# Decoder layer on one Trainium2 core: scratch tiles for two pairs, a token-shift mix on ScalarE, and convolution splits and evacuations at high priority

## The chip, the core and the metric

The kernel runs on one core of a Trainium2 chip. The metric is the device time of one execution, in microseconds. TensorE (PE) does the matrix products, VectorE (DVE), ScalarE (ACT) and GpSimd (POOL) the elementwise work, and the queue of SyncE (SP) issues nearly all loads.

## The reference, cut to what matters

One layer of a decoder on 256 prompt tokens and 8 sequences of 4 new tokens (288 columns in all). The part that matters here:

```python
proj = h @ w_in                                   # columns: r, k, v, then bg, cg, hc
rkv = p_rkv + (p_rkv_prev - p_rkv) * mu_rkv       # mix with the token before
decay = exp(-exp(w_log)); a = sigmoid(...)        # two small low-rank products
kk = k * k_k / max(|k * k_k|, 1e-12)
k = k * (1 + (a - 1) * k_a)
y, S = wkv7_scan(state, r, decay, k, v, kk, kk * a)    # delta rule, 16 heads
zc = causal_dwconv(state_conv, cg * hc, conv_w)        # width 3
o_conv = bg * zc
x = x + ga1 * (concat(o_rwkv, o_conv) @ w_out)
# then a gated feed-forward part and a last norm
```

## The kernel before, in words

Activations lie with features on the 128 partitions and 288 tokens in the free dimension. Every large product is made of three passes (`mm3`, lines 163 to 166): a piece of weights of 1 MB (`raw`) is split into a high part (`whi`, a cast on ScalarE, line 154) and a low part (`wlo`, a subtraction on VectorE, line 156), and TensorE does high x high, high x low and low x high, 128x288 each. There are four tiles for `raw` in the stage that matters here and three each for `whi` and `wlo`.

The kernel has these stages: setup and the r, k, v columns of `w_in` (to about 268 us), then the stage of this change, then the scan for eight pairs of heads (`second(p)`), then `w_out`, the feed-forward part and the end.

The stage of this change (lines 555 to 731) goes over the eight pairs of heads p. For each it does `lerp` (the mix of r, k and v with the token before, three of them), `first(p)` (the preparation of the scan: line 599 is its product on TensorE), and `blocks_of(p - 1)` (small products, lines 635 and 637, whose results go to memory in HBM as `dN` and `dNs`). All their temporary tiles are turns of rings in one scratch tile, `ws`: two `ldr` tiles for `lerp` and eight `er` tiles for `first`, which uses seven of them for one pair.

Between these, generators are stepped. `cv` is the convolution's own product over 2048 features: 24 steps, each with one piece of 1 MB, two splits and 48 passes of 128x288 (6.3 us by the profile). Two steps make one part, and `conv_evac` then takes the two accumulators out. `rest` is the product for the adaLN vectors that later stages need; one step loads 1 MB and takes four passes of 128x512 side by side (lines 298 and 301).

After the last pair, `substitute()` reads `dN` and `dNs` back, does a forward substitution on VectorE and GpSimd (lines 664 and 665, 31 steps that depend on each other), and writes the result to memory (`dT`, `dTT`, `dTs`). `second(0)` reads that back into `T1` and `TTc` (lines 994 to 998). Then `drain(cv)` runs what is left of the convolution.

The code is ordered by a scheduler: within its program order and priorities it fixes the order of the instructions on each engine before the run, and on the chip each engine keeps to that order.

## Time and profile before

| | |
|---|---|
| median of 3 runs | 1697.93 us (1694.07 to 1701.84) |
| the profiled execution | 1694.01 us, span 1692.2 us |
| TensorE busy | 1630.8 us, 96% of the span |
| VectorE, ScalarE, GpSimd busy | 1160.7, 713.6, 387.1 us |
| TensorE clock granted, mean | 0.983 |

The span is what the trace covers, 1.8 us less than the execution's time. A busy TensorE is not one at its peak, since passes overlap in the records; the number of passes in a stretch tells more. The granted clock is 1.00 at 2.4 GHz and 0.5 at 1.2 GHz, and a value between is a mean over a stretch that had both.

### The profile page before, as it was taken

What the parts mean: (1) busy time and instruction counts of PE and PEld (TensorE: products, weight loads), DVE (VectorE), ACT (ScalarE), POOL (GpSimd) and SP (SyncE); (2) the same over time, 40 slices, a digit from 0 to 9 for tenths busy, and PEclk for the clock granted to TensorE, in tenths of its full rate; (3) what the DMA queues carried; (4) which work ended last, traced back from release to release, by engine and by line L of the source; (5) the groups of instructions that cost most, each with busy time, mean ns of one, the idle gap of its engine ahead of it and who ended that gap; (6) DMA issues with size and microseconds to landing.
All of it is one profiled execution on the core that took longest, in us unless ns stands there. A gap on an engine that the chain in (4) does not pass through costs nothing.

```text
span 1692.2 us, 32395 instructions
## 1 busy us (share of the span) xinstructions
PE 1630.8 (96%) x12713; PEld 1481.5 (88%) x12713; DVE 1160.7 (69%) x2464; ACT 713.6 (42%) x1281; POOL 387.1 (23%) x853
## 2 busy tenths in 40 slices
PE   6999999999889999899899999999999999999996
PEld 3778898889866666699799999999999999999996
DVE  3687798977846665554776676757676766757586
ACT  4543355444234433333654343443434343434444
POOL 2132011221633232100143031221213131221212
PEclk9999999999979999999999999999999999999998
DMA  8897865688567667954654545545545445445532
GB/s 274 287 334 270 281 214 191 198 254 258 160 181 248 215 232 247 331 175 141 224 175 150 175 157 168 174 152 173 163 162 174 151 150 183 166 156 169 174 125 76
DMA packets 238306, 333.61 MB, mean 197 GB/s; under 512 B 35698, under 2 KB 180826, under 8 KB 229546
## 3 DMA queue, kind: packets, MB, share of 16 engines
q1 hardware_dynamic: 234937, 324.55, 58.8%
q0 software_dynamic: 2848, 6.20, 1.1%
q8 instruction: 100, 1.64, 0.4%
q10 hardware_dynamic: 368, 0.79, 0.2%
q14 instruction: 53, 0.43, 0.1%
HBM read 321.63 MB, written 9.89 MB: 196 GB/s over the span
## 4 chain that ended last, share of the span: by engine, by line
PE 84%; DVE 8%; ACT 3%; DMA 2%; POOL 1%; issue 1%; SPq 0%; DVEq 0%; ACTq 0%
PE acc L164 22%; PE acc L166 22%; PE acc L165 22%; PE ada L298 5%; DVE wlo L156 2%; PE acc L298 2%; ACT whi L154 1%; PE wb L298 1%; PE wa L298 1%; PE acc L301 1%; PE wa L301 1%; PE ada L301 1%; DMA A<-in_x_sample_dram 1%; PE wb L164 1%; PE wb L166 0%
## 5 line engine op out<-in xcount | busy, mean ns | idle before, releaser
L164 PE MATMUL acc<-actH,whi 128*128 128x288 f32 (+1 forms) x2368 | 707.1, 299 | 9.0 <-ACT whi L154 5.2
L165 PE MATMUL acc<-actL,whi 128*128 128x288 f32 (+1 forms) x2368 | 703.6, 297 | 0.1
L166 PE MATMUL acc<-actH,wlo 128*128 128x288 f32 (+1 forms) x2368 | 700.9, 297 | 2.8 <-DVE wlo L156 2.7
L156 DVE TENSOR_TENSOR wlo<-raw,whi 128x1024 fp32r<-128x1024 f32 (+1 forms) x391 | 478.6, 1226 | 217.3 <-ACT whi L154 211.0
L154 ACT CAST whi<-raw 128x1024 fp32r<-128x1024 f32 x400 | 417.6, 1048 | 475.9 <-PE acc L165 409.3
L164 PEld LDWEIGHTS acc<-actH,whi 128*128 128x128 f32 x2368 | 448.6, 189 | 20.2 <-ACT whi L154 9.7
L166 PEld LDWEIGHTS acc<-actH,wlo 128*128 128x128 f32 x2368 | 447.8, 190 | 5.6 <-DVE wlo L156 4.6
L165 PEld LDWEIGHTS acc<-actL,whi 128*128 128x128 f32 x2368 | 448.3, 189 | 0.4 <-DVE actL L161 0.3
L164 PE MATMUL acc<-gH,whi 128*128 128x288 f32 x704 | 209.1, 297 | 1.7 <-DVE rd L1051 1.7
L166 PE MATMUL acc<-gH,wlo 128*128 128x288 f32 x704 | 210.4, 299 | 0.0
L165 PE MATMUL acc<-gL,whi 128*128 128x288 f32 x704 | 205.7, 292 | 0.0
L1144 POOL COPY uO<-ub 128x2 f32<-128x2 f32 x88 | 24.6, 280 | 548.6 <-ACT ub L1142 548.6
L164 PEld LDWEIGHTS acc<-gH,whi 128*128 128x128 f32 x704 | 132.3, 188 | 3.8 <-PE acc L166 3.7
L165 PEld LDWEIGHTS acc<-gL,whi 128*128 128x128 f32 x704 | 134.0, 190 | 0.0
L166 PEld LDWEIGHTS acc<-gH,wlo 128*128 128x128 f32 x704 | 132.0, 187 | 0.7
L1049 DVE SCALAR_TENSOR_TENSOR xT<-acc,modT,xT 128x256 f32<-128x256 f32 x192 | 91.7, 477 | 27.6 <-PE acc L166 27.6
L301 PE MATMUL ada<-raw,cT 128*32 128x512 f32 x576 | 109.3, 623 | 0.0
L298 PE MATMUL ada<-raw,cT 128*32 128x512 f32 x192 | 100.0, 623 | 1.0 <-DMA raw<-in_ada_w_dram 0.7
L1149 DVE SCALAR_TENSOR_TENSOR uz<-ub,cw,uz 128x304 f32<-128x304 f32 x176 | 96.5, 548 | 4.3
L1141 POOL COPY ub<-sF 128x16 f32<-128x16 f32 x88 | 71.2, 809 | 103.9 <-ACT sF L1045 103.9
L1147 DVE TENSOR_SCALAR uz<-ub,cw 128x304 f32<-128x304 f32 x88 | 33.1, 376 | 49.5 <-ACT ub L1143 49.5
L463 DVE TENSOR_TENSOR A<-acc,A 128x296 f32<-128x296 f32 x96 | 44.2, 463 | 29.0 <-PE acc L166 28.5
(449 smaller groups left out, 1985.0 us busy)
## 6 DMA issues: line engine op xcount, KB each, us to landing
raw<-in_ada_w_dram SPq DMA_DIRECT2D x88, 1024.0 KB, 5.2
raw<-in_ffn_up_dram SPq DMA_DIRECT2D x88, 1024.0 KB, 5.1
raw<-in_w_in_dram SPq DMA_DIRECT2D x48, 1024.0 KB, 7.4
raw<-in_ffn_down_dram SPq DMA_DIRECT2D x44, 1024.0 KB, 5.2
raw<-in_w_out_dram SPq DMA_DIRECT2D x16, 1024.0 KB, 5.9
raw<-in_ada_w_dram SPq DMA_DIRECT2D x16, 512.0 KB, 8.0
dX<-xT SPq DMA_DIRECT2D x1, 2304.0 KB, 16.0
xT<-dX POOLq DMA_DIRECT2D x4, 576.0 KB, 9.3
```

The costliest lines, as they stand in the source:

```text
L154: S.copy(hi, raw)
L156: (GP if cur['share'] and cur['turns'] % cur['share'] == 0 else V).tensor_tensor(lo, raw, hi.bitcast(F32), SUB)
L164: E.matmul(acc, wh, xh, start=start, stop=False)
L165: E.matmul(acc, wh, xl, start=False, stop=False)
L166: E.matmul(acc, wl, xh, start=False, stop=stop)
L298: ins = calls[0]().ins
L301: c()
L463: V.tensor_tensor(A[:, t, 2:LW], acc[:, :NL], A[:, t, 2:LW], ADD)
L1049: V.scalar_tensor_tensor(xT[:, t, :T0], acc[:, :T0], modT[:, m, t, 0:1], xT[:, t, :T0], MUL, ADD)
L1141: GP.tensor_copy(bv[:, :, 0:2], sF[:, :, j].rearrange("p (b t) -> p b t", t=2))
L1147: V.tensor_scalar(z[:, :NC - 2], b[:, 0:NC - 2], cw[:, 0, j:j + 1], None, MUL)
L1149: V.scalar_tensor_tensor(z[:, :NC - 2], b[:, t:NC - 2 + t], cw[:, t, j:j + 1], z[:, :NC - 2], MUL, ADD)
```

## The change

It has five parts, all in the stage of the pairs.

- `lerp` computes the mix in another form: (1 - mu) times the tile plus mu times the tile shifted by one. The two multiplications and a small one for the first tokens of the 8 sequences go to ScalarE (lines 583 to 585 of the changed file), one addition stays on VectorE (line 586). The new constant `omur` is made once.
- One scaling in `first` (line 619) and the first tap of the convolution (line 706) go from VectorE to ScalarE.
- The rings `ldr` and `er` have four and sixteen tiles. The ten new ones lie where the substitution's tiles `UL`, `TL` and `TTL` lie.
- The splits of the convolution and its evacuations are placed under `high_priority`, so the scheduler takes them first on their engines.
- The loop over the pairs steps `cv` once and not twice, so 8 of the 24 steps come before `substitute()` in the program and 16 after.

```diff
-            ldr, off = ring(0, (NT,), 2)
-            er, off = ring(off, (NT,), 8)
+            ld_, off = views(0, *[(NT,)] * 2)
+            e_, off = views(off, *[(NT,)] * 8)
...
+            more, _ = views(off + NP * NT, *[(NT,)] * 10)
+            (ocv, UL, TL, TTL, ULs, TTs), off = views(off, (NP, NT), (32, 32), (32, 32), (32, 32), (TS, TS), (TS, TS))
+            ldr, er = turns(ld_ + more[8:]), turns(e_ + more[:8])
...
-                d = ldr()
-                before(d, A[:, t])
-                V.scalar_tensor_tensor(A[:, t, 2:2 + NT], d, murkv[:, t:t + 1], A[:, t, 2:2 + NT], MUL, ADD)
+                a, d, mu = A[:, t], ldr(), murkv[:, t:t + 1]
+                S.activation(d, a[:, 1:1 + NT], AF.Copy, scale=mu)
+                S.activation(s4(d[:, T0:])[:, :, 0], a[:, 2 + NT:LW], AF.Copy, scale=mu)
+                S.activation(a[:, 2:2 + NT], a[:, 2:2 + NT], AF.Copy, scale=omur[:, t:t + 1])
+                V.tensor_tensor(a[:, 2:2 + NT], a[:, 2:2 + NT], d, ADD)
...
-                V.tensor_scalar(a, a, kav[:, p:p + 1], omka[:, p:p + 1], MUL, ADD)
+                S.activation(a, a, AF.Identity, scale=kav[:, p:p + 1], bias=omka[:, p:p + 1])
...
-                                    hv, lv = split(raw[:, kk:kk + 4], 4)
+                                    with tc.high_priority():
+                                        hv, lv = split(raw[:, kk:kk + 4], 4)
...
-                        for n in range(2):
-                            conv_evac(part, 2 * jj + n, accs[n], cg[:, n], z[n])
+                        with tc.high_priority():
+                            for n in range(2):
+                                conv_evac(part, 2 * jj + n, accs[n], cg[:, n], z[n])
...
-                    V.tensor_scalar(z[:, :NC - 2], zb[:, 0:NC - 2], cwv[:, j:j + 1], None, MUL)
+                    S.activation(z[:, :NC - 2], zb[:, 0:NC - 2], AF.Copy, scale=cwv[:, j:j + 1])
...
                 step(cv)
-                step(cv)
```

On TensorE, the place around the products of the last pair (`blocks_of(7)`: lines 635 and 637 before, 645 and 647 in the changed file, where line numbers are up to 12 higher; `ada` is the adaLN product, `acc` a pass of the convolution). Before:

```order
L166 MATMUL acc<-actH,wlo 128x288
L298 MATMUL ada<-raw,cT 32x512
L301 MATMUL ada<-raw,cT 32x512 x3
L298 MATMUL ada<-raw,cT 32x512
L301 MATMUL ada<-raw,cT 32x512 x3
L635 MATMUL wb<-XA,XB 64x64 x4
L637 MATMUL wb<-XA,XB 32x32
L635 MATMUL wa<-XA,XB 64x64 x4
L637 MATMUL wa<-XA,XB 32x32
L164 MATMUL acc<-actH,whi 128x288
```

and in the changed kernel:

```order
L166 MATMUL acc<-actH,wlo 128x288
L299 MATMUL ada<-raw,cT 32x512
L302 MATMUL ada<-raw,cT 32x512 x3
L299 MATMUL ada<-raw,cT 32x512
L302 MATMUL ada<-raw,cT 32x512 x3
L645 MATMUL wb<-XA,XB 64x64 x4
L647 MATMUL wb<-XA,XB 32x32
L645 MATMUL wa<-XA,XB 64x64 x4
L647 MATMUL wa<-XA,XB 32x32
L262 MATMUL ada<-con,ada_sb 128x128 x4
L164 MATMUL acc<-actH,whi 128x288
```

The rows read alike; what moved is the work around them. Before, 768 passes of the convolution stand ahead of these products (96 for each pair) and 384 behind them; now it is 384 ahead (16 to 59 between one pair's products and the next) and 768 behind. The number of `ada` steps ahead of them is 16 in both.

On VectorE and ScalarE, the place where the first pairs' mixes are made, behind the two splits for the low-rank weights. On VectorE before (line 341 the shifted difference, 342 its small part, 576 the mix, 611 and 612 already `first`):

```order
L161 TENSOR_TENSOR wlo<-raw,whi 96x1024 x2
L342 TENSOR_TENSOR ws<-A 128x8 x2
L611 SCALAR_TENSOR_TENSOR ws<-con,XA 128x288
L576 SCALAR_TENSOR_TENSOR A<-ws,vec,A 128x288 x2
L341 TENSOR_TENSOR ws<-A 128x288
L612 TENSOR_TENSOR ws<-ws,XA 128x288
L342 TENSOR_TENSOR ws<-A 128x8
L156 TENSOR_TENSOR wlo<-raw,whi 128x1024
```

and on ScalarE now (583 to 585 the three multiplications of a mix, 607 the first step of `first`):

```order
L154 CAST whi<-raw 128x1024
L583 ACTIVATE ws<-A,vec 128x288 x2
L584 ACTIVATE ws<-A,vec 128x8
L585 ACTIVATE A<-A,omur 128x288
L584 ACTIVATE ws<-A,vec 128x8
L585 ACTIVATE A<-A,omur 128x288
L583 ACTIVATE ws<-A,vec 128x288
L154 CAST whi<-raw 128x1024
L584 ACTIVATE ws<-A,vec 128x8
L585 ACTIVATE A<-A,omur 128x288
L607 ACTIVATE ws<-A,vec 128x288
```

Where VectorE had three instructions for each of the 24 mixes, ScalarE now has three and VectorE one addition.

On SyncE's queue, the place where the last pair's results go out and come back for the substitution (`dN`, `dNs` out: lines 651 and 652; back into `ws`: 658 and 663; `in_w_in` are pieces for the convolution, `in_ada_w` for `rest`). In the changed kernel:

```order
L253 DMA raw<-in_ada_w_dram 128x2048
L651 DMA dNs<-ws 32x4 x2
L170 DMA raw<-in_w_in_dram 128x8x256
L652 DMA dN<-ws 128x4x64
L651 DMA dNs<-ws 32x4 x2
L170 DMA raw<-in_w_in_dram 128x8x256
L658 DMA ws<-dNs 64x16 x2
L663 DMA ws<-dN 32x32x32 x4
L170 DMA raw<-in_w_in_dram 128x8x256 x14
```

Now 14 loads of the convolution stand behind these transfers in the queue; before, there were four. For every two `in_ada_w` pieces of the pairs the queue now has one convolution piece, where before it had two.

## Rows read from the trace of the kernel before

**Rows 1.** The page: span, and busy time of TensorE.

```profile
span 1692.2 us, 32395 instructions
...
PE 1630.8 (96%) x12713; PEld 1481.5 (88%) x12713; DVE 1160.7 (69%) x2464; ACT 713.6 (42%) x1281; POOL 387.1 (23%) x853
```

**Rows 2.** Stretches of the stage: width, busy (instructions), TensorE clock, DMA share, GB/s.

```profile
268.00:300.00 32.00, 28.61 (x213) 25.20 (x212) 31.53 (x71) 22.23 (x43) 6.95 (x14) 1.00 0.60 202
300.00:415.00 115.00, 115.00 (x912) 100.03 (x910) 95.27 (x199) 51.15 (x87) 28.74 (x53) 1.00 0.75 238
415.00:441.00 26.00, 26.00 (x197) 25.84 (x197) 18.97 (x48) 6.68 (x8) 9.89 (x29) 1.00 0.88 254
441.00:466.00 25.00, 20.07 (x128) 19.58 (x127) 23.77 (x53) 8.80 (x11) 17.13 (x33) 0.87 0.27 91
475.00:503.60 28.60, 24.65 (x238) 17.68 (x237) 11.62 (x38) 10.53 (x29) 9.78 (x33) 0.64 0.78 194
```

**Rows 3.** What TensorE waited for, 268 to 512 us: total, times, longest us.

```profile
PE acc L164 <- DVE ws L703: 3.8, 1, 3.8
PE acc L301 <- DMA T<-dT: 2.7, 1, 2.7
PE acc L166 <- DVE wlo L156: 2.7, 2, 1.6
```

**Rows 4.** The chain of waits, 310 to 350 us: start, us, what.

```profile
328.33 0.68 PE wa L599 x2
...
345.37 0.68 PE wb L599 x2
```

**Rows 5.** TensorE in order of time: start, us, line, operation, tiles.

```profile
268.12 0.62 PE L298 MATMUL ada<-raw,cT 128*32 128x512 f32 x1
...
414.88 0.24 PE L637 MATMUL wa<-XA,XB 64*32 64x32 f32 x2
...
475.04 0.62 PE L298 MATMUL ada<-raw,cT 128*32 128x512 f32 x1
...
522.22 0.43 PE L892 MATMUL wa<-AX,ws 128*128 128x64 f32 x2
```

**Rows 6.** The chain of waits, 474 to 512 us.

```profile
474.36 2.06 ACT ws L666
...
476.44 4.21 DMA dT<-ws
...
490.94 0.62 PE wa L892 x2
```

**Rows 7.** Groups of instructions, 268 to 415 us: busy us, mean ns, idle before.

```profile
L156 DVE TENSOR_TENSOR wlo<-raw,whi 128x1024 fp32r<-128x1024 f32 x35 | 43.6, 1257 | 14.1 <-ACT whi L154 13.9
...
L154 ACT CAST whi<-raw 128x1024 fp32r<-128x1024 f32 x35 | 36.0, 1046 | 23.6 <-PE acc L165 12.5 <-DMA raw<-in_w_in_dram 6.7 <-DVE ws L616 2.1
...
L576 DVE SCALAR_TENSOR_TENSOR A<-ws,vec,A 128x288 f32<-128x288 f32 x24 | 13.6, 576 | 0.1
...
L341 DVE TENSOR_TENSOR ws<-A 128x288 f32<-128x288 f32 x24 | 10.5, 450 | 0.0
...
L342 DVE TENSOR_TENSOR ws<-A 128x8 f32<-128x8 f32 x24 | 5.9, 259 | 0.0
...
L597 ACT ACTIVATE ws<-A,vec 128x288 f32<-128x288 f32 x8 | 4.3, 536 | 13.4 <-POOL A L622 13.3
```

**Rows 8.** VectorE in order of time: the first step of the substitution.

```profile
430.61 0.21 DVE L664 TENSOR_TENSOR ws<-ws 128x3 f32<-128x3 f32 x1
```

**Rows 9.** SyncE in order of time: the next four weight loads.

```profile
426.83 7.63 SPq L170 DMA_DIRECT2D raw<-in_w_in_dram  x4
```

**Rows 10.** Stretches of the stage before, columns as in rows 2.

```profile
42.00:100.00 58.00, 57.17 (x412) 46.27 (x412) 37.07 (x83) 27.90 (x55) 8.62 (x14) 0.99 0.89 311
100.00:200.00 100.00, 97.71 (x717) 83.44 (x716) 80.62 (x174) 39.81 (x64) 20.58 (x32) 1.00 0.81 277
```

**Rows 11.** Line 892, one pair after another: duration, first and last start us.

```profile
L892 PE MATMUL wa<-AX,ws x16: 275/323/473, 490.9 to 675.5; 128*128 128x64 f32 x16
```

More of the change, by code (lines that the diff above doesn't have):

```diff
@@ L184 @@
     omka = cst.tile([P, NP], F32, name="omka")
+    omur = cst.tile([P, 24], F32, name="omur")
     actx = ctx.enter_context(ExitStack())
@@ L470 @@
                         V.tensor_scalar(omka, kav, -1.0, 1.0, MUL, ADD)
+                        V.tensor_scalar(omur, murkv, -1.0, 1.0, MUL, ADD)
                         setup.close()
@@ L547, in ring, with turns @@
             aps, off = views(off, *[shape] * n)
+            return turns(aps), off
+        def turns(aps):
             count = [0]
@@ L551, in turn @@
                 count[0] += 1
-                return aps[count[0] % n]
-            return turn, off
+                return aps[count[0] % len(aps)]
+            return turn
         if True:
-            ldr, off = ring(0, (NT,), 2)
-            er, off = ring(off, (NT,), 8)
+            ld_, off = views(0, *[(NT,)] * 2)
+            e_, off = views(off, *[(NT,)] * 8)
             ntr, off = ring(off, (4, CL), 2)
@@ L563 @@
             zbr, off = ring(off, (NC,), 1)
-            (ocv, UL, ULs, TL, TTL, TTs), off = views(off, (NP, NT), (32, 32), (TS, TS), (32, 32), (32, 32), (TS, TS))
+            more, _ = views(off + NP * NT, *[(NT,)] * 10)
+            (ocv, UL, TL, TTL, ULs, TTs), off = views(off, (NP, NT), (32, 32), (32, 32), (32, 32), (TS, TS), (TS, TS))
+            ldr, er = turns(ld_ + more[8:]), turns(e_ + more[:8])
             st, off = ring(off, (256,), 1)
```

## The prediction

> **What bounds the kernel now.** I read the page first. TensorE is busy for 96% of the span [rows 1], so little can be gained but in stretches where it idles or runs at half clock. So I next cut the stage of the pairs into stretches [rows 2]. In the middle one, 300 to 415 us, TensorE is busy for all 115 us at full clock, although VectorE is at 95.27 / 115 = 83%: nothing that only relieves VectorE there can be worth anything. The stage loses time at three other places. From 268 to 300 us TensorE idles 3.4 us while VectorE is full (31.53 of 32). From 441 to 466 us it idles 4.9 us and the clock is 0.87. From 475 to 503.6 us the clock is 0.64, and it idles 4.0 us.
>
> Who is waited for is in the third view [rows 3]: once 3.8 us for an evacuation of the convolution (line 703, on VectorE), once 2.7 us for `T1`, which comes back from memory, and twice for a low part. The first and second have one cause, the substitution. It begins at 430.6 us [rows 8], some 16 us after the last pair's products at 414.88 [rows 5], and takes VectorE until the copy behind it starts at 474.36; the chain then goes through the transfer to memory at 476.44 and on into `second(0)` [rows 6]. The convolution ends at 475.04 [rows 5], just as the substitution does, so nothing is left to cover the way through memory.
>
> **The change, part by part.** First the cadence. 415 to 441 us holds 197 passes in 26 us: 0.132 us a pass [rows 2]. A pair takes 345.37 - 328.33 = 17.04 us [rows 4], of which 96 passes are 12.67; so what else a pair asks of TensorE (two adaLN steps, line 599, the small products) is 4.37 us.
>
> *One convolution step for each pair.* From the stage's start (268.1) to the last pair's products TensorE's own work is 16 x 3 low-rank passes (6.3 us), 8 x 4.37 = 35.0 and the convolution. Before: 101.4 for 768 passes, in all 142.7, against 146.8 on the trace; the difference is about the idle 3.4. After: 50.7 for 384 passes, in all 92.0. Behind the last pair stand now 768 passes (101.4), before 384 (50.7). By TensorE's work alone the convolution would end at 268.1 + 92.0 + 101.4 + 0.4 (a transposition) = 461.9, that is 13.1 us earlier than 475.0: these are the idle and half-clock microseconds of rows 2.
>
> The substitution is hidden by this. Before, from the last pair's products to its end were 474.4 - 414.9 = 59.5 us, splits and evacuations among it included. If it takes as long again, and the way through memory another 490.9 - 474.4 = 16.5, all is there 76 us after the pairs, and the convolution needs 101.4. Without this cover the 16.5 us would stand between the convolution and `second(0)`, as they partly do now.
>
> *What the shorter loop asks of the others.* Loads first. From 268 us to the last pair the queue has to bring some 24 pieces of 1.05 MB (16 adaLN steps, 8 of the convolution, as many ahead at the end as at the start) and eight times 0.13 MB for `dN` go out: 26.2 MB. At 238 GB/s the DMA engines were 0.75 busy [rows 2], so 317 GB/s is full; that makes 82.6 us at full share. Full share isn't seen: with TensorE near 98% busy the stage before had 0.89 over 58 us and 0.81 over 100 us [rows 10]. So the loop takes 93 us at 0.89, 102 at 0.81 and 110 at 0.75. TensorE wants 92. I take 97.5, midway between the first two, since a four-tile ring with two kinds of loads is nearer to these than to a stage that asked for less.
>
> *ScalarE.* It was busy 22.2 + 51.2 = 73.4 us in the old loop [rows 2], with 35 casts of 1.046 [rows 7]. It loses 19 casts (19.9 us). Each mix adds two activations of 128x288 with a scale for each partition, which line 597 has at 0.536 us, and one of 128x8, which I bound by VectorE's 0.259 below and 0.536 above, and take at 0.26: 24 x 1.33 = 32.0 us (38.6 at the upper bound). Line 619's successor and the first taps are 10 more of 0.536 (5.4). Sum: 90.9 us, or 97.5. It is under the 97.5 us taken, but not by much.
>
> *VectorE.* It loses 24 x (0.576 + 0.450 + 0.259) = 30.8 us and gains 24 additions of 0.450 (10.8), and 19 splits of 1.257 go behind the loop (23.9): from 126.8 us to 83 at most. It is no bound; an addition waits for ScalarE's second multiplication, and `first` of later pairs and the splits are queued behind it.
>
> *Scratch tiles.* They cost nothing by themselves. A pair's seven tiles no longer wait for those of the pair before. The tiles lie on `TTL`, so its clearing on GpSimd waits for pair 7's mixes; GpSimd was busy 35.7 of 147 us [rows 2], which covers it.
>
> *Priority.* The evacuation that TensorE awaited for 3.8 us goes ahead of the substitution on VectorE. That wait is counted in the 13.1.
>
> *Behind the last pair.* SyncE's queue first reads `dN` and `dNs` back, and before the next weight loads then left at 426.8 us [rows 9], 12 us after the products. Two pieces (12.7 us of TensorE) lie ahead. If the queue is as late again, a landing and a split put TensorE's stall at some 8 us; if the pair's few small copies go first, as the order has it, at nothing. I take 3.
>
> *The start of `second(0)`.* It loses the wait of 2.7 us. The half clock costs more: from pair 0 to pair 1 line 892 takes 522.2 - 490.9 = 31.3 us [rows 5, 6], and later (675.5 - 522.2) / 6 = 25.6 [rows 5, 11]; 5.7 us more. Whether the clock falls again I can't read: the small products of `second(0)` stand alone on TensorE in both orders, only without the wait for memory. Bounds 2.7 and 8.4; I take 5.
>
> **Sum.** The convolution ends at 268.1 + 97.5 + 0.4 + 101.4 + 3 = 470.4, which is 4.6 us earlier, and with 5 of `second(0)` 9.6 are gained. The rest of the program is the same. The span becomes 1682.6 and the execution 1694.0 - 9.6 = 1684.4. This execution lies 3.9 under the median of the runs shown (1697.93), so I forecast 1688.
>
> **The rivals.**
>
> *The gain is whole.* The loads run at 0.89, the loop takes 93, no stall behind the last pair, and the clock stays up in `second(0)`: the convolution ends at 462.9, 12.1 + 8.4 = 20.5 us are gained, 1677. For it: TensorE's short waits in 268 to 300 us never pulled the clock down [rows 2]. Against it: the loop then wants every engine above 90%.
>
> *The loads hold the loop.* At the share of 0.75 which the old loop had, it takes 110 us (with 0.4 + 101.4 and no more stall than 0 to 3 the convolution ends at 480 to 483), and with 5 of `second(0)` back the time is 1698 to 1701: no change. For it: the queue is served in order, and the small transfers of each pair stand between the loads. The break-even is a loop of 107 us.
>
> *ScalarE becomes the bound.* With 90.9 us at the 83% that VectorE had in the old loop, it takes 109.5 us: 1700, no change. Against it: when VectorE alone was the bound, it was full to 98.5%, and ScalarE would then need 92. The Trainium skill (ScalarE: Activation LUTs, Rules for kernel authors) has a rule against this part: adds and multiplies belong on VectorE, not ScalarE. By this rule the first two parts of the change work against each other; the trace agrees as to the price (0.536 on ScalarE against 0.450 for an addition), not as to which engine is short, since VectorE is the full one from 268 to 300 us.
>
> *Slower.* The shares above are of loops that TensorE set. If two kinds of loads in a ring of four, with TensorE taking both adaLN tiles only where its order has them, reach no more than 0.70, the loop takes 118 us, TensorE waits in pieces for 26, and the clock may fall in them. The convolution ends at 491, and with 5 back it is 11 us slower: 1709. It decides from a loop of 116 us on (0.71), where the loss passes 0.5%. For it: 268 to 300 us ran at 0.60 [rows 2]. Against it: there VectorE was the bound.
>
> **How the numbers follow.** Half a per cent, 8.5 us, is about what a measurement can tell here from no change. The forecast has 0.45: its loops of 94 to 101 us give 13 to 6 us, and those under 98.6, two thirds of them, give more than 8.5. The whole gain has 0.18, the loads at 0.75 have 0.14, ScalarE 0.11, slower 0.12. So faster is 0.30 + 0.18 = 0.48, the same 0.15 + 0.25 = 0.40, slower 0.12. The range goes from the whole gain (1677) to 1703, which takes in both cases of no change and leaves the slower one out. The forecast's own range is 1685 to 1692.
>
> **What would show it.** Right: the last pair's products at about 366 us (now 415), the first line of the substitution some 16 us behind them, its last well before the convolution ends at about 470, no wait of TensorE for `T1`, and no wait for an evacuation. The loop's DMA share would be about 0.85. Wrong in the loop: TensorE waits for casts of pieces that a load releases (the loads), or for `XB` and low parts while ScalarE is above 95% (ScalarE). Wrong behind it: a wait for a cast some 12 us after the last pair, or the clock at half from `second(0)`'s start for 20 us again. What I trust least is the 97.5: it is a mean between two shares of a stage with another mix of loads.

## The result, and the profile after

The changed kernel is slower: 1716.51 us median (1711.86 to 1719.30, 4 runs) against 1696.00 us for the kernel before beside it (1686.58 to 1701.84, 4 runs), a ratio of 1.0125 with an interval of 1.0079 to 1.0170. The forecast was 1688, within 1677 to 1703. Its profiled execution took 1714.68 us. The first rows of its page answer to [rows 1]: the span is 20.7 us longer, and TensorE's share is again 96%, so the page alone doesn't say where the time went.

```profile
span 1712.9 us, 32443 instructions
...
PE 1637.1 (96%) x12713; PEld 1487.6 (87%) x12713; DVE 1144.5 (67%) x2401; ACT 746.0 (44%) x1369; POOL 380.8 (22%) x853
```

In this stage the lines of the changed kernel stand 10 to 12 further down than before: the pair's products are 645 and 647, the substitution's steps 674 and 675, the evacuations of the convolution's second part 714 and 715, its taps 718 (now on ScalarE) and 720, the evacuations of the third part 723 and 724. TensorE in order of time shows the same marks as [rows 5]: the last products of a pair, the end of the convolution (the adaLN pass behind it), pair 0 and pair 1 of the scan.

```profile
373.99 0.24 PE L647 MATMUL wa<-XA,XB 64*32 64x32 f32 x2
...
502.61 0.62 PE L299 MATMUL ada<-raw,cT 128*32 128x512 f32 x1
...
515.75 0.69 PE L903 MATMUL wa<-AX,ws 128*128 128x64 f32 x2
...
543.76 0.43 PE L903 MATMUL wa<-AX,ws 128*128 128x64 f32 x2
```

The loop of pairs is 41 us shorter, but behind it the convolution takes 128.6 us instead of 60.2 (128.8 and 60.4 from the last large product of that pair, 0.15 us before the row shown; the sums below count from there), and ends 27.6 us later. Pair 0 comes 24.8 us later, pair 1 only 21.5: here some is given back. The stretches of the stage (columns as in [rows 2]) say where TensorE loses it.

```profile
268.00:300.00 32.00, 30.70 (x233) 26.59 (x232) 21.62 (x36) 28.23 (x62) 5.67 (x12) 0.98 0.76 262
300.00:374.00 74.00, 67.78 (x516) 53.58 (x515) 60.07 (x141) 54.59 (x129) 25.75 (x45) 0.92 0.70 213
374.00:412.00 38.00, 24.43 (x137) 23.34 (x136) 24.03 (x55) 9.33 (x11) 14.20 (x35) 0.73 0.70 184
412.00:441.00 29.00, 25.71 (x183) 25.51 (x183) 22.21 (x51) 9.97 (x10) 11.61 (x23) 0.94 0.50 158
441.00:503.00 62.00, 62.00 (x464) 61.10 (x467) 32.43 (x50) 24.22 (x35) 5.09 (x23) 1.00 0.46 148
503.00:538.00 35.00, 33.49 (x367) 22.96 (x359) 18.18 (x57) 15.94 (x51) 13.52 (x43) 0.85 0.77 232
```

From 374 to 412 us, just behind the last pair, TensorE idles for 13.6 of 38 us at a mean clock of 0.73, and VectorE, the next, is busy for only 24.0, ScalarE for 9.3. Such a picture is one of engines that wait for each other. The loop itself (300 to 374) is no longer full either. From 441 us on, when the substitution is over, all is well.

What TensorE waited for, first in the loop (268 to 374 us), then behind it (374 to 505 us); total, times, longest us:

```profile
PE wb L645 <- POOL XB L631: 4.5, 3, 1.6
PE acc L164 <- ACT whi L154: 1.8, 1, 1.8
PE acc L166 <- DVE wlo L156: 0.8, 1, 0.8
PE ada L299 <- DMA raw<-in_ada_w_dram: 0.5, 1, 0.5
```

```profile
PE acc L166 <- DVE wlo L156: 8.4, 2, 6.9
PE acc L164 <- ACT whi L154: 5.2, 2, 4.2
PE acc L164 <- DVE ws L724: 3.3, 1, 3.3
```

Behind the last pair these are 16.9 us. TensorE's own work there is 768 passes and a transposition, 101.8 us, so 27.0 are lost. Of the other 10 some 8 go with the clock, which was at its lower level for about 24 us (38 x 0.27 x 2 and 29 x 0.06 x 2): TensorE was busy for 16.2 of these with 65 passes, 8.6 us of work at the full level. In the loop the waits are 7.6 us, and some 13 us at the lower clock cost up to half of that.

VectorE in order of time shows how the long waits arise:

```profile
385.30 2.36 DVE L156 TENSOR_TENSOR wlo<-raw,whi 128x1024 fp32r<-128x1024 f32 x2 [0.33 <-ACT whi L154]
...
388.36 0.16 DVE L675 TENSOR_TENSOR ws<-ws 128x3 f32<-128x3 f32 x1
392.88 0.42 DVE L714 TENSOR_TENSOR ws<-acc,ws 128x256 f32<-128x256 f32 x1 [4.36 <-PE acc L166]
...
394.03 1.11 DVE L720 SCALAR_TENSOR_TENSOR ws<-ws,vec 128x304 f32<-128x304 f32 x2 [0.62 <-ACT ws L718]
...
397.55 0.21 DVE L674 TENSOR_TENSOR ws<-ws 128x31 f32<-128x31 f32 x1
...
403.48 0.46 DVE L675 TENSOR_TENSOR ws<-ws 128x192 f32<-128x192 f32 x1
403.86 1.48 DVE L156 TENSOR_TENSOR wlo<-raw,whi 128x1024 fp32r<-128x1024 f32 x1
```

And ScalarE and TensorE in the same stretch:

```profile
384.21 2.00 ACT L154 CAST whi<-raw 128x1024 fp32r<-128x1024 f32 x2 [7.56 <-DMA raw<-in_w_in_dram]
...
393.44 0.55 ACT L718 ACTIVATE ws<-ws,vec 128x304 f32<-128x304 f32 x1 [7.23 <-DVE ws L715]
395.94 0.55 ACT L718 ACTIVATE ws<-ws,vec 128x304 f32<-128x304 f32 x1 [1.95 <-POOL coO L716]
396.40 2.92 ACT L154 CAST whi<-raw 128x1024 fp32r<-128x1024 f32 x3
```

```profile
392.95 0.29 PE L166 MATMUL acc<-actH,wlo 128*128 128x288 f32 x1
397.48 0.40 PE L164 MATMUL acc<-actH,whi 128*128 128x288 f32 x1 [4.23 <-ACT whi L154]
...
405.40 0.85 PE L166 MATMUL acc<-actH,wlo 128*128 128x288 f32 x2 [6.89 <-DVE wlo L156]
```

The waits follow each other in a ring. At 388.5 us VectorE comes to an evacuation (714), which in its fixed order stands ahead of the next splits, and waits 4.36 us for TensorE to finish those sums. When TensorE has finished them, at about 392.9, it wants the next weights at once. Their casts stand on ScalarE behind two taps, and these wait for VectorE's evacuations: 4.2 us. The low part then stands on VectorE behind the taps and 16 instructions of the substitution (397.55 to 403.9): 6.9 us more. None of these long waits goes back to a load: the cast that waited for one, until 384.21, was done at 385.3, and TensorE came to it at 386.7. At 398 us the clock falls to the lower of its two levels (1.2 instead of 2.4 GHz) and stays there for 13.7 us.

### The profile page after: what moved, and what is told of

It reads as the page before. It is cut to its first block, busy times and chain, and to the rows that moved or that the text cites. A ratio compares the mean times of both kernels' runs of the same rounds, so it can differ in the third digit from the quotient of the medians.

```text
span 1712.9 us, 32443 instructions
## 1 busy us (share of the span) xinstructions
PE 1637.1 (96%) x12713; PEld 1487.6 (87%) x12713; DVE 1144.5 (67%) x2401; ACT 746.0 (44%) x1369; POOL 380.8 (22%) x853
## 4 chain that ended last, share of the span: by engine, by line
PE 83%; DVE 8%; ACT 3%; DMA 2%; issue 1%; POOL 1%; SPq 0%; DVEq 0%; ACTq 0%; POOLq 0%
PE acc L164 22%; PE acc L166 22%; PE acc L165 22%; PE ada L299 4%; DVE wlo L156 2%; PE acc L299 2%; ACT whi L154 1%; PE wb L299 1%; PE wa L299 1%; PE acc L302 1%; PE wa L302 1%; PE ada L302 1%; PE wb L164 1%; PE wb L166 1%; DMA A<-in_x_sample_dram 1%
## 5 line engine op out<-in xcount | busy, mean ns | idle before, releaser
L164 PEld LDWEIGHTS acc<-actH,whi 128*128 128x128 f32 x2368 | 451.8, 191 | 29.3 <-ACT whi L154 15.7
L166 PEld LDWEIGHTS acc<-actH,wlo 128*128 128x128 f32 x2368 | 450.8, 191 | 13.0 <-DVE wlo L156 11.6
L1060 DVE SCALAR_TENSOR_TENSOR xT<-acc,modT,xT 128x256 f32<-128x256 f32 x192 | 91.8, 478 | 27.6 <-PE acc L166 27.6
L1153 ACT COPY ub<-acc 128x256 f32<-128x256 f32 x84 | 31.7, 378 | 75.6 <-PE acc L166 75.6
## 6 DMA issues: line engine op xcount, KB each, us to landing
dX<-xT SPq DMA_DIRECT2D x1, 2304.0 KB, 14.9
```

The costliest lines, as they stand in the source:

```text
L164: E.matmul(acc, wh, xh, start=start, stop=False)
L166: E.matmul(acc, wl, xh, start=False, stop=stop)
L1060: V.scalar_tensor_tensor(xT[:, t, :T0], acc[:, :T0], modT[:, m, t, 0:1], xT[:, t, :T0], MUL, ADD)
L1153: S.copy(b[:, 2:258], acc[:, :T0])
```

## The experiments

Theory A: the loss is made by the pacing. Sixteen instead of eight convolution steps lie behind the last pair, and their splits share VectorE's fixed order with the substitution. Theory B: it is made by the other parts, the taps on ScalarE and the evacuations put first, wherever the steps lie. All runs are set together here. "Lost" is the time not covered by TensorE's own work: in the loop (from 268.1 us), what exceeds 41.3 us (the prediction's 6.3 and 35.0) and 0.132 us for each convolution pass in it (up to 33 of these are the last of the r, k, v columns); behind it, what exceeds 0.4 us and 0.132 for each pass. In six kernels a part of the 41.3 us lies elsewhere, ahead of 268.1 us (e2, e3, e12, e14, e15) or behind the last pair (e3, e16). It is counted where it lies, at 0.132 us for a low-rank pass and 0.43 for four adaLN passes. The ratio of times is to runs of the kernel before beside it, with its interval.

| kernel | last pair, us | convolution ends, us | lost in the loop | lost behind it | ratio |
|---|---|---|---|---|---|
| before | 414.7 | 475.1 | 4.0 | 9.3 | 1 |
| changed | 373.8 | 502.7 | 12.6 | 27.1 | 1.0125 (1.0079 to 1.0170) |
| e1, two steps | 414.7 | 473.8 | 2.4 | 8.0 | 0.9976 (0.9956 to 0.9996) |
| e17, the same again | 416.6 | 475.6 | 3.7 | 7.9 | 1.0007 (0.9983 to 1.0030) |
| e2, one step alone | 376.1 | 492.8 | 19.3 | 14.9 | 1.0107 (1.0077 to 1.0136) |
| e3, no priority | 361.1 | 493.6 | 13.4 | 22.7 | 1.0071 (1.0042 to 1.0100) |
| e4, tap on VectorE | 372.6 | 501.1 | 10.9 | 26.8 | 1.0112 (1.0079 to 1.0145) |
| e5, one step of the substitution | 375.3 | 495.7 | 11.9 | 18.6 | 1.0088 (1.0061 to 1.0115) |
| e12, no step of it | 370.1 | 478.7 | 11.7 | 6.8 | 1.0030 (1.0006 to 1.0053) |
| e6, substitution later | 373.9 | 491.1 | 12.1 | 15.4 | 1.0080 (1.0037 to 1.0123) |
| e7, mixed steps | 404.2 | 481.9 | 3.7 | 14.0 | 1.0018 (0.9998 to 1.0038) |
| e10, mixed, substitution later | 405.8 | 484.8 | 5.1 | 15.3 | 1.0012 (0.9988 to 1.0036) |
| e11, as e10, products later | 399.6 | 481.3 | 0.1 | 18.0 | 1.0005 (0.9984 to 1.0026) |
| e8, mix on VectorE | 377.5 | 495.2 | 15.7 | 16.0 | 1.0083 (1.0049 to 1.0117) |
| e9, products later | 377.8 | 506.6 | 16.4 | 27.1 | 1.0134 (1.0096 to 1.0171) |
| e13, addition on GpSimd | 382.2 | 498.3 | 19.5 | 14.4 | 1.0102 (1.0060 to 1.0145) |
| e14, e13 with two steps | 417.5 | 476.4 | 8.6 | 7.9 | 1.0019 (0.9995 to 1.0044) |
| e15, no addition | 369.3 | 485.5 | 12.8 | 14.4 | 1.0075 (1.0048 to 1.0101) |
| e16, no multiplication | 370.8 | 501.3 | 14.4 | 20.7 | 1.0149 (1.0111 to 1.0187) |

### Which part of the change costs the time

e1 undoes the pacing alone; e2 makes it alone, on the kernel before.

```
 # e1, from the changed kernel
                 step(cv)
+                step(cv)
 # e2, from the kernel before
                 step(cv)
-                step(cv)
```

> The changed kernel with two convolution steps for each pair again, all else as changed. Theory A (pacing): with one step a pair, 16 of the convolution's 24 steps instead of 8 lie behind the last pair, and their splits and evacuations then share VectorE's fixed order with the substitution; the some 17 us of TensorE's waits and the half clock after them come from this. Then two steps give all of it back: the last pair's products at about 415 us, the convolution's end at 471 to 478 us, the time 1686 to 1697. Theory B (round trips): the first tap on ScalarE and the evacuations put first make VectorE and ScalarE wait for TensorE and for each other, wherever they stand. Then the waits stay, earlier or later, and the time is 1703 to 1712.

> The kernel before with one convolution step for each pair, nothing else changed (no scratch tiles, no mix or taps on ScalarE, no priority). Theory A (pacing): it shows the same loss as the changed kernel, TensorE waiting for splits that stand behind steps of the substitution on VectorE, behind the last pair 120 us or more up to the convolution's end; the time is 1706 to 1720. Theory B (round trips): behind the last pair no wait over 3 us, and the time is 1690 to 1700.

Theory A holds both ways. With two steps the loss is gone, in e1 and again in e17; with one step alone nearly all of it is there, 1.0107. One of A's numbers is missed: from the last pair to the convolution's end e2 takes 116.7 us, where A had 120 or more. What TensorE waited for in e2, 372 to 505 us:

```profile
PE acc L166 <- DVE wlo L156: 5.2, 2, 4.6
PE acc L164 <- DVE ws L712: 1.5, 1, 1.5
```

The waits are of the same kinds as in the changed kernel, but shorter; with the other parts they are longer behind the last pair (27.1 against 14.9 us lost) and the loop is better (12.6 against 19.3).

> The changed kernel with two steps for each pair, as before in this study. If its lead of 0.24% over the kernel before is real, the ratio is 0.996 to 0.999 again; if it was scatter, 0.999 to 1.002.

The 0.24% by which e1 led isn't found again: the scratch tiles, the mix on ScalarE and the priority together make no difference that these runs can tell, once the pacing is undone. Nor does the priority do in e1 what it was made for. The evacuation for which the kernel before lost 3.8 us [rows 3] stands behind steps of the substitution (674, 675) again, and TensorE waits 3.9 us for it:

```profile
458.98 0.27 DVE L675 TENSOR_TENSOR ws<-ws 128x104 f32<-128x104 f32 x1
459.16 0.42 DVE L714 TENSOR_TENSOR ws<-acc,ws 128x256 f32<-128x256 f32 x1
```

```profile
459.83 0.58 PE L164 MATMUL acc<-actH,whi 128*128 128x288 f32 x1 [3.93 <-DVE ws L715]
```

e3 takes the priority away, e4 puts the first tap back.

```
 # e3, from the changed kernel
-                                    with tc.high_priority():
-                                        hv, lv = split(raw[:, kk:kk + 4], 4)
+                                    hv, lv = split(raw[:, kk:kk + 4], 4)
...
-                        with tc.high_priority():
-                            for n in range(2):
-                                conv_evac(part, 2 * jj + n, accs[n], cg[:, n], z[n])
+                        for n in range(2):
+                            conv_evac(part, 2 * jj + n, accs[n], cg[:, n], z[n])
 # e4, from the changed kernel
-                    S.activation(z[:, :NC - 2], zb[:, 0:NC - 2], AF.Copy, scale=cwv[:, j:j + 1])
+                    V.tensor_scalar(z[:, :NC - 2], zb[:, 0:NC - 2], cwv[:, j:j + 1], None, MUL)
```

> The changed kernel without priority for splits and evacuations. Theory A (pacing): the convolution's splits and evacuations stand behind the substitution's steps with or without priority, so the loss stays, 1710 to 1722. Theory B (round trips): without priority the evacuations no longer stand ahead of work that could run, VectorE's wait of 4.4 us for TensorE's accumulators at 388 us goes, and the time falls to 1698 to 1706. A third theory, that the priority did help as predicted, gives 1722 or more.

> The changed kernel with the convolution's first tap on VectorE again, as before the change. Theory A (pacing): 1710 to 1718, the long wait of TensorE for the split behind 16 steps of the substitution stays; the casts no longer stand behind the taps on ScalarE, which gives back the wait of 4.2 us at 393 us at most. Theory B (round trips): the waits at 393 us and 398 us both go, and with them the half clock, 1698 to 1705.

e3 misses the numbers of all three theories: its median of 1709.0 lies between A's and B's. Its loop loses about as much (13.4 us, with 336 passes in it instead of 393), and behind the last pair 22.7 are lost instead of 27.1. So the priority didn't help, as the prediction had it, and may have hurt; its ratio and the changed kernel's overlap. e4 is A's. The wait for casts is gone, as expected, but the low part is then late by as much more:

```profile
PE acc L166 <- DVE wlo L156: 12.3, 2, 10.8
PE acc L164 <- DVE ws L724: 4.9, 1, 4.9
PE acc L164 <- ACT whi L154: 0.9, 1, 0.9
```

So the taps on ScalarE pass VectorE's wait on; they don't make it.

### What holds VectorE's queue

e5 keeps only the substitution's first step, e12 none. Read-backs, clearings, copies and transfers stay in both; the multiplications and additions are left out.

```
 # e5, from the changed kernel
                             if hi > lo:
                                 tv = turn()[:, :m * (hi - lo)].rearrange("p (b a) -> p b a", a=m)
-                                eng.tensor_tensor(tv, ex(W[:, lo:hi, s], m), exf(U[:, s, s + 1:n], hi - lo), MUL)
...
+                                if s == 0:
+                                    eng.tensor_tensor(tv, ex(W[:, lo:hi, s], m), exf(U[:, s, s + 1:n], hi - lo), MUL)
...
 # e12, from the changed kernel
-                    for s in range(n - 1):
-                        m = n - 1 - s
...
-                                eng.tensor_tensor(W[:, lo:hi, s + 1:n], W[:, lo:hi, s + 1:n], tv, ADD)
```

> The changed kernel with the substitution cut to its first step (its other 37 multiplications and additions on each engine are left out, so the output is another; all loads, clearings, copies and transfers stay). Theory A1 (shared queue): TensorE's waits behind the last pair are for splits and evacuations that stand behind the substitution's steps in VectorE's fixed order. Without them the convolution ends 102 to 107 us after the last pair's products (changed kernel 128.8) and the time is 1688 to 1695. Theory A2 (weights): the pieces themselves come late, since SyncE's queue carries the pairs' small transfers between the loads. Then the waits stay as waits for casts, behind the last pair it takes 115 us or more, and the time is above 1700.

> The changed kernel without any of the substitution's multiplications and additions, on VectorE and on GpSimd (left out; its read-backs, clearings, copies and transfers stay, the output is another). Theory A1 (VectorE's fixed order): whatever waits at the head of VectorE's queue behind the last pair holds the splits behind it; with the single step still in place that was the step itself, 5.9 us for its read-back. Without a step only the evacuations are left, which need TensorE alone: behind the last pair 102 to 110 us (changed kernel 128.8, with one step 120.4), the time 1690 to 1699. Theory A2 (weights late, or ScalarE's taps ahead of the casts): a wait for a cast of over 4 us stays, behind the last pair 115 us or more, the time above 1702.

e5 missed: 18.6 us are still lost behind the last pair, and the wait is now for a cast. The waits of all engines from 372 to 420 us:

```profile
PE acc L164 <- ACT whi L154: 9.5, 2, 8.4
...
DVE ws L675 <- DMA ws<-dNs: 5.9, 1, 5.9
...
DVE ws L715 <- PE acc L166: 4.8, 1, 4.8
```

The step that was left (675 here) waits on VectorE 5.9 us for its data to come back from memory, but this isn't what TensorE lacks: the wait ends at 386.5 us, and the cast of the next split ends only at 386.9, since it waited for a load. What is left is the ring. VectorE waits 4.8 us at the evacuation (715) for TensorE, the taps on ScalarE (719) wait for the evacuations, and the casts stand behind the taps and behind a copy of the substitution's result (677):

```profile
385.90 2.00 ACT L154 CAST whi<-raw 128x1024 fp32r<-128x1024 f32 x2 [7.60 <-DMA raw<-in_w_in_dram]
...
399.38 1.92 ACT L677 COPY ws<-ws 64x1024 f32<-64x1024 f32 x1 [1.58 <-DVE ws L676]
...
401.94 2.94 ACT L154 CAST whi<-raw 128x1024 fp32r<-128x1024 f32 x3 [0.63 <-ACT ws L677]
```

In e12, which has no step, 108.6 us pass behind the last pair, 6.8 are lost instead of 27.1, and one wait is above 1 us, of 2.5. But e12 differs from e5 in more than the step. One more piece of the convolution is loaded ahead of the read-backs, and on VectorE six splits and not four stand ahead of the first evacuation (706 here), which then hardly waits:

```profile
388.14 0.42 DVE L706 TENSOR_TENSOR ws<-acc,ws 128x256 f32<-128x256 f32 x1 [0.60 <-PE acc L166]
```

The other traces tell the two apart. Of the kernels that take one step for each pair and the whole substitution ahead of the steps that are left, three have four splits ahead of that evacuation (the changed one, e4 and e9). VectorE waits there for 4.1 to 4.4 us, and 26.8 to 27.1 us are lost behind the last pair. Four have six splits (e2, e8, e13 and e15); VectorE waits there for 0.2 us at most, and 14.4 to 16.0 are lost. (e3 and e16 are in neither group: they have one convolution step more behind the last pair, eight and seven splits and steps of the substitution ahead of the first evacuation, and TensorE waits for the evacuations themselves, 2.6 and 3.9 us in e3, 3.4 and 4.1 in e16.) Without the steps it is 18.6 with four splits (e5) and 6.8 with six (e12). So by these comparisons the evacuation's place is worth some 12 us, and the steps of the substitution some 8. Theory A1 holds in its wider form, that whatever waits at the head of VectorE's queue holds the splits behind it. Late weights (A2) make none of the changed kernel's long waits, as its rows show; that they have no part in the order was not tested. And e12 takes 1.003 of the time of before even so, with the substitution left out: the loop of one step loses 11.7 us by itself.

e6 leaves no work out and changes only the place at which the substitution is written.

```
+            for _ in range(6):
+                step(cv)
             substitute()
             drain(cv)
```

> The changed kernel, with the substitution written behind 6 of the 16 convolution steps that are left, instead of ahead of all; no work is left out. Theory A1 (shared queue): the first splits behind the last pair stand ahead of the substitution's steps, TensorE's waits of 4.2 and 6.9 us at 393 and 398 us go, with the half clock after them, and the substitution still ends before the convolution; behind the last pair 106 to 114 us, the time 1695 to 1703. Theory A2 (weights): behind the last pair 120 us or more, 1708 to 1718.

The waits of 4.2 and 6.9 us are gone and the convolution ends 11.6 us earlier; 117.2 us behind the last pair and a time of 1705.4 lie between the numbers of A1 (114 and 1703 at most) and A2 (120 and 1708 at least), so neither is met. Here too six splits stand ahead of the first evacuation. One wait of 4.3 us is left, for an evacuation that is now behind steps of the substitution (674), at a later place:

```profile
PE acc L164 <- DVE ws L674: 4.3, 1, 4.3
PE acc L166 <- DVE wlo L156: 2.4, 3, 0.9
```

### Mixed pacing

e7 takes two steps for six pairs and one for two; e10 also writes the substitution behind 4 of the 10 steps left; e11 also takes the products two pairs behind (its edit is e9's, below).

```
 # e7, from the changed kernel
                 step(cv)
+                if p < 6:
+                    step(cv)
 # e10, from e7
+            for _ in range(4):
+                step(cv)
             substitute()
```

> The changed kernel with two convolution steps for pairs 0 to 5 and one for pairs 6 and 7: 14 of 24 steps lie in the loop, 10 behind it. Theory A1 (shared queue): the loss grows with the number of steps in which TensorE needs a split at once while the substitution runs. With two steps more behind the last pair than in the kernel before, the substitution's end is covered, TensorE doesn't wait for T1, and of the 27 us lost behind the last pair at most 10 come back: 1686 to 1700. If pacing of the last pairs alone is what hurts (the splits of the pieces ahead are used up when the substitution begins), it is 1703 to 1714.

> The changed kernel with both remedies: two convolution steps for pairs 0 to 5 and one for 6 and 7, and the substitution written behind 4 of the 10 steps that are left. If the loss is made by splits that stand behind the substitution just as TensorE needs them, the wait of 5 us at 428 us that the mixed pacing alone still has goes, the convolution ends at 471 to 476 us, second(0) keeps the 6 us that it got back, and the time is 1686 to 1692, faster than the kernel before. If the mixed pacing loses its time elsewhere, the time is 1694 to 1699, as with the mixed pacing alone.

> The kernel with both remedies (mixed pacing, substitution behind 4 of 10 steps), and the pairs' small products two pairs behind their scans. By theory L1 (chain within a pair) the loop loses its waits for XB as well, the last pair's products end 2 to 4 us earlier, and the time is 1683 to 1690. By theory L2 nothing changes against the kernel with both remedies (within 2 us).

All three come out level with the kernel before, none ahead. With 14 steps in the loop 14.0 us are lost behind it, with 16 steps 8.0: two steps more behind the last pair cost 6.0 us, and from the convolution's end on only 2.4 come back (1214.7 us to the end, before 1217.1). In e10 the wait for the low part is shorter (3.2 instead of 4.9), but a new one has come at 465 us (waits from 400 to 490 us):

```profile
PE acc L164 <- DVE ws L817: 5.1, 1, 5.1
PE acc L166 <- DVE wlo L156: 3.8, 3, 3.2
```

The profile names line 817, a copy of the stage that follows. But the evacuation (714, 715) ended at 470.17 us, 0.15 ahead of the pass that waited, as in e1, so this is again a wait for an evacuation. On VectorE it stands behind a split that waited 2.99 us for its cast. e11 has the best loop of all, 0.1 us lost, and gives it back behind it, 18.0 lost. What one place gains, the next one of the same fixed order takes.

### What makes the loop of one step longer than forecast

It took 105.7 us, not 97.5; 1.2 us of this are nine passes of the r, k, v columns, which end a little later here. Six kernels, each from the changed kernel:

```
 # e8
-                a, d, mu = A[:, t], ldr(), murkv[:, t:t + 1]
...
-                V.tensor_tensor(a[:, 2:2 + NT], a[:, 2:2 + NT], d, ADD)
+                d = ldr()
+                before(d, A[:, t])
+                V.scalar_tensor_tensor(A[:, t, 2:2 + NT], d, murkv[:, t:t + 1], A[:, t, 2:2 + NT], MUL, ADD)
 # e9
-                if p:
-                    blocks_of(p - 1)
+                if p > 1:
+                    blocks_of(p - 2)
...
+            blocks_of(NP - 2)
             blocks_of(NP - 1)
 # e13 (e14: and a second step(cv))
-                V.tensor_tensor(a[:, 2:2 + NT], a[:, 2:2 + NT], d, ADD)
+                GP.tensor_tensor(a[:, 2:2 + NT], a[:, 2:2 + NT], d, ADD)
 # e15
-                V.tensor_tensor(a[:, 2:2 + NT], a[:, 2:2 + NT], d, ADD)
 # e16
-                S.activation(a[:, 2:2 + NT], a[:, 2:2 + NT], AF.Copy, scale=omur[:, t:t + 1])
```

> The changed kernel with the shifted mix on VectorE again, as before the change. It says which engine sets the loop of pairs, 105.7 us in the changed kernel against the 97.5 forecast. If ScalarE sets it (rival of the prediction), the loop gets shorter, 97 to 101 us, and the time is 1707 to 1713. If the mix on ScalarE relieves the engine that is short, VectorE, the loop takes 110 us or more, 1718 to 1726. If neither (a chain of short waits within each pair), it stays within 3 us of 105.7 and the time at 1713 to 1720.

> The changed kernel, with each pair's small products (the function blocks_of) taken two pairs behind its own scans instead of one. It asks what makes the loop 105.7 us where 97.5 was forecast. Theory L1 (chain within a pair): TensorE reaches a pair's products before GpSimd has written XB, waits three times 1.5 us, and the half clock that follows costs as much again; with a pair more between them the waits for XB go and the loop takes 97 to 101 us; the time 1706 to 1713. Theory L2 (casts and loads): TensorE finds the next wait at once, for a cast or a low part, and the loop stays at 103 us or more, 1712 to 1719.

> The changed kernel with the mix's last addition on GpSimd instead of VectorE, 24 instructions; nothing is left out. Theory L3 (VectorE bounds the loop, with all it has to do within a pair): it loses 24 x 0.45 = 10.8 us there, and the loop takes 97 to 100 us instead of 105.7, the waits for XB get shorter; the time 1706 to 1712. Theory L1 (a chain over VectorE, ScalarE and GpSimd within a pair): GpSimd takes some 0.70 us for an addition of this shape and stands in the chain, so the loop takes 105 us or more and the time is 1715 to 1724.

> The changed kernel with two convolution steps for each pair again, and the mix's last addition on GpSimd. With two steps TensorE sets the loop from 300 us on, so VectorE's relief is worth something only from 268 to 300 us, where TensorE idled 3.4 us in the kernel before: up to 3 us against the changed kernel with two steps, 1689 to 1695. If the substitution's place behind the last pair decides alone, no difference, 1692 to 1697.

> The changed kernel without the mix's last addition (24 instructions on VectorE left out, so the output is another). Theory L3 (VectorE bounds the loop with one step a pair): 10.8 us less on VectorE, the loop takes 95 to 99 us instead of 105.7 and the time is 1704 to 1711. Theory L4 (ScalarE bounds it): the loop stays at 103 us or more, 1712 to 1718.

> The changed kernel without the mix's multiplication by one minus mu in place (24 activations of some 0.53 us on ScalarE, 12.7 us, left out, so the output is another). Theory L4 (ScalarE bounds the loop): the loop takes 94 to 99 us, the time is 1702 to 1711. Theory L3 (VectorE): the loop stays at 103 us or more, 1712 to 1718. If both this and the kernel without the addition have shorter loops, it is the chain through both engines, not the load of one.

The expectations split here, and only e9's second (L2) is borne out by its numbers. In e8 the loop takes 109.4 us (counted from 268.1, as all here), and 15.7 are lost in it instead of 12.6; so the mix on ScalarE is no loss in the loop, and ScalarE doesn't set it. The 11 us that e8 has back behind the last pair come with the six splits ahead of the first evacuation. In e9 the three short waits for `XB` gave way to one of 7.1 us: the loop doesn't get shorter, as L2 had it, but it is `XB` itself that is late, not a cast. Without the addition on VectorE (e15, 10.8 us less) the last pair comes 4.5 us earlier (a loop of 101.2), without the multiplication on ScalarE (e16, 12.6 us less) 3.1 (102.7). But in both, TensorE has 4.8 us less work of its own between 268.1 us and the last pair. In e15, 14 low-rank and 16 adaLN passes lie ahead of that mark, as do the nine of the r, k, v columns; in e16, 48 passes of the convolution and 16 of adaLN have moved behind the loop, and 24 more of the r, k, v columns lie in it. Lost are 12.8 and 14.4 us, against 12.6. So the load of neither engine is the bound by itself. e16's text asked for two shorter loops as the sign of a chain through both engines, and neither is shorter; what sets the loop stays open.

e13 was to relieve VectorE and slowed it. Groups of instructions, 268 to 385 us, in the changed kernel and then in e13 (busy us, mean ns, idle before):

```profile
L616 DVE TENSOR_TENSOR ws<-ws 128x288 f32<-128x288 f32 x8 | 4.1, 515 | 0.1
...
L627 DVE SCALAR_TENSOR_TENSOR XA<-ws 128x288 f32<-128x288 f32 x8 | 3.7, 464 | 0.1
```

```profile
L616 DVE TENSOR_TENSOR ws<-ws 128x288 f32<-128x288 f32 x8 | 5.5, 691 | 0.2
...
L627 DVE SCALAR_TENSOR_TENSOR XA<-ws 128x288 f32<-128x288 f32 x8 | 5.0, 626 | 0.2
...
L586 POOL TENSOR_TENSOR A<-A,ws 128x288 f32<-128x288 f32 x24 | 22.9, 967 | 32.1 <-ACT A L585 32.1
```

These instructions take a third longer, and the moved addition takes 0.97 us; the last pair comes 8.4 us later, with 19.5 us lost in the loop. So e13 tells nothing of VectorE as the bound, and e15 asked that again. e14 has no lead over e1 and e17.

## Why the prediction was wrong

**"Behind the last pair ... I take 3", bounds 0 to 8.** This step failed. The term was mis-sized by 24: it measured 27.0 us. It counted only a landing and a split behind SyncE's transfers. It left out that splits and evacuations share one fixed order with the substitution on VectorE, and that TensorE now needs each split soon after it is made, since no lead is left from the loop: the first low part behind the last pair was ready 3.4 us ahead of its pass in the kernel before (412.0 and 415.4 us), and 0.1 in the changed one (378.0 and 378.1). By the comparisons under e12, some 12 of the 27 us come with the evacuation that stands ahead of the next splits and some 8 with the substitution's steps; 6.8 are lost without either. The half clock behind the waits (some 8 of the 27) wasn't in the bounds either.

**"The evacuation that TensorE awaited for 3.8 us goes ahead of the substitution."** This step failed too. The first evacuation behind the last pair goes ahead of most of the substitution, and that is what hurts: VectorE waited 4.36 us at it with everything behind it. The next ones stand behind the substitution's steps all the same: TensorE waited 3.3 us for one in the changed kernel, and 3.9 in e1. e3, without priority, was no slower.

**"The substitution is hidden by this."** Right in the narrow sense: it ended at 433.3 us, 69 us ahead of the convolution, and no wait for `T1` is left. The passes that hid it are the ones that lost the time.

**The loop, 97.5 us.** The direction was right, the size wrong: 105.7, the second term that failed, by 8.2. The loads, from which the number was worked out, weren't the limit: TensorE waited 0.5 us for one in all the loop, at a share of 0.70 to 0.76. Busy times came out as forecast (VectorE 81.7 us for "83 at most", ScalarE 82.8 for 90.9), but with these two engines at 77 and 78% of the 106 us TensorE wasn't full: it waited 7.6 us in short pieces, 4.5 of them for `XB`. The short waits pulled the clock down three times, which the whole-gain rival had taken as excluded by 268 to 300 us of before.

**ScalarE as the bound** was a rival, and e8 and e16 speak against it. The rule of the Trainium skill that stood there (ScalarE: Activation LUTs, Rules for kernel authors) asks for adds and multiplies on VectorE; by it e8 should have the shorter loop, and it has the longer one, 109.4 against 105.7 us, though the whole of e8 isn't slower. The runs here don't agree with the rule for this loop.

**second(0), 5 us back.** Right, and a little more: from the convolution's end to the end of the span it takes 1210.2 us instead of 1217.1, 6.9 less, and 6 of these are there by pair 1. The clock at its start is 0.85 from 503 to 538 us, where it was 0.64 [rows 2].

**The slower rival** had the right sign by another mechanism: loads at a share of 0.70 and a loop of 118 us. The share was 0.70 to 0.76 and the loop 105.7. By the prediction's own form, 268.1 + 105.7 + 0.4 + 101.4 + 27.0 is 502.6, where the convolution ended.

## What to carry to other kernels

Work that is moved from a stage where TensorE is full to one where a serial chain holds another engine's queue loses its lead there: ask of each instruction of the chain what stands behind it in that queue, and who wants it at once. An instruction that stands early in an in-order queue helps only if its inputs are ready by then; if they come from the engine that is starved, it closes a ring. Taking a wait away at one place of such an order isn't yet a gain: e9, e10 and e11 each removed one and met it again at the next place. And before loops of two kernels are compared from a fixed time, count the work in them: two of the loops here looked shorter because some of it lay outside.

## What the runs showed of the hardware

VectorE's instructions took longer beside GpSimd's in e13. Line 616, both inputs in SBUF, took 0.96 us at 356.28, beside a GpSimd addition at 356.23, and 0.46 us at 367.88 with GpSimd idle:

```profile
356.28 0.96 DVE L616 TENSOR_TENSOR ws<-ws 128x288 f32<-128x288 f32 x1
...
367.88 0.46 DVE L616 TENSOR_TENSOR ws<-ws 128x288 f32<-128x288 f32 x1
```

```profile
356.23 0.69 POOL L586 TENSOR_TENSOR A<-A,ws 128x288 f32<-128x288 f32 x1 [1.44 <-ACT A L585]
```

The Trainium skill (SBUF — State Buffer, SBUF: two separate sides) says that a VectorE instruction with two SBUF inputs and a GpSimd instruction that reads SBUF exclude each other for the whole instruction. These rows agree in the main: 0.96 is the rest of the GpSimd addition (0.64 us) and 0.32 more, a little under the sum of 0.64 and 0.46.

TensorE's clock fell at short waits too: in the loop of the changed kernel none was longer than 1.8 us, and the mean clock from 300 to 374 us was 0.92, where the loop of before had 1.00 [rows 2]. And in a stage that no kernel here changes it was at 0.87 from 600 to 680 us in the profiles of e2, e10, e11 and e13 (0.94 in e7 and e8), at 1.00 in those of the kernel before and of e12, with TensorE busy for 78.4 to 78.6 of the 80 us in each. From the convolution's end to the end of the program these four took 1218.5 to 1219.3 us, the changed kernel and e12 1210.2 and 1210.9. No cause was found, so the spans of single profiles are compared here up to the convolution's end, and whole kernels by their medians.
